# Two loads on two queues in place of one, for the last 15 full loads of a row-mean kernel

## The chip, the cores and the metric

The kernel runs on one core of one Trainium2 chip. The metric is the time of one execution on the device, in microseconds (us). Times named below are medians of several executions; a profile is one further execution, with its own time.

## The reference

```python
def setup_inputs():
    return {"x": np.random.randn(64, 256, 8192).astype(np.float32)}

def reference(x):
    return np.mean(x, axis=2)
```

There are 64 x 256 = 16,384 rows of 8,192 float32 (32 KB each), 536.87 MB in all, and one mean for each row comes out.

## The kernel before

**Rows and partitions.** Each of the 128 SBUF partitions owns 128 rows (`OWN`), in three zones of 95, 17 and 16 rows per partition. `rows_of(n, k)` is the slice of x with the own rows n to n+k-1 of every partition; in a zone these lie one behind the other in memory, so a slice of two rows is one run of 64 KB for each partition.

**Loads and buffers.** There are 63 full loads (`NB`), numbered g = 0 to 62. Each brings two rows per partition (128 x 64 KB, 8.39 MB) into one of three buffers, `bufs[g % 3]`, 64 KB per partition each. Load 0 comes in three pieces (lines 108 to 112), loads 1 and 2 at line 114, loads 3 to 47 in a loop of 15 rounds of three (line 121), and loads 48 to 62 one by one (line 127). All are issued by SyncE (SP) on its DMA queue. Before load g is issued, SP waits until the reduction of load g-3 has freed the buffer (`free_sems`).

**Reductions.** VectorE (DVE) waits for load g (`in_sems`), sums its two rows in one tensor_reduce of 128 x 16384 and frees the buffer. Loads 0 to 59 are reduced in a loop (line 168), loads 60 and 61 at line 178, and load 62 as two halves-sums (line 151, one for each row) that tell `owned_sem` when they are done.

**The tail.** The last two rows of each partition come in five chunks, which get smaller (line 133): 4,560, 2,240, 768, 368 and 256 KB. SP issues all five once load 60 has been reduced; the first four go into buffer 0, the last into `fin`. DVE sums the first chunk's full row and its own share of the next ones (line 151), ScalarE (ACT) sums its own share of the first four (line 207), and one last DVE sum over `fin` gives the last mean. GpSimd (POOL, line 97) scales all other sums once `owned_sem` has reached 4, that is after the two halves-sums of load 62, the reduction of load 61 and the sum of the first chunk's row. SP then issues the two stores of `scaled` (line 136), waits for the last DVE sum and issues the store of `ends` (line 140).

**Order.** Every engine runs its own list in the order written. ACT has nothing to do before the first chunk has landed; its list begins with the loading of its function table. The semaphores named are the only ties between engines.

## Time and profile before

| | |
|---|---|
| Median of 3 executions | 1243.22 us (1243.2 to 1243.32) |
| The profiled execution's own time | 1243.06 us |
| Its span, first to last instruction | 1241.7 us |
| Input read | 536.87 MB, 432 GB/s over the span |
| DVE busy | 1084.1 us (87%) |
| ACT busy | 5.2 us |
| POOL busy | 2.9 us |

What lies between the span and the execution's own time is 1.36 us. Engine names in the profile: DVE is VectorE, ACT is ScalarE, POOL is GpSimd, SPq is SyncE's list of DMA issues. "L168" is line 168 of the kernel. A row of the timeline gives start, duration, engine, line, operation, output<-input with partitions x elements, and in square brackets how long the engine had been idle and what ended that. The DMA share is the mean busy share of 16 DMA engines; a packet is one piece of a transfer that the profile records on one of them.

### The profile page before, as it was taken

What the parts mean: (1) busy time and instruction counts of PE and PEld (TensorE: products, weight loads), DVE (VectorE), ACT (ScalarE), POOL (GpSimd) and SP (SyncE); (2) the same over time, 40 slices, a digit from 0 to 9 for tenths busy, and PEclk for the clock granted to TensorE, in tenths of its full rate; (3) what the DMA queues carried; (4) which work ended last, traced back from release to release, by engine and by line L of the source; (5) the groups of instructions that cost most, each with busy time, mean ns of one, the idle gap of its engine ahead of it and who ended that gap; (6) DMA issues with size and microseconds to landing.
All of it is one profiled execution on the core that took longest, in us unless ns stands there. A gap on an engine that the chain in (4) does not pass through costs nothing. (4 is left out here: it accounts for less than half of the span.)

```text
span 1241.7 us, 549 instructions
## 1 busy us (share of the span) xinstructions
DVE 1084.1 (87%) x76; ACT 5.2 (0%) x9; POOL 2.9 (0%) x9
## 2 busy tenths in 40 slices
DVE  2898988989889898898898988989889898898987
ACT  0000000000000000000000000000000000000001
POOL 0000000000000000000000000000000000000000
DMA  9999999999999999999999999999999999999998
GB/s 405 439 439 439 439 435 410 439 439 439 439 439 433 412 439 439 439 439 439 426 418 439 439 439 439 439 422 422 439 439 439 439 439 422 422 439 439 439 439 374
DMA packets 10512, 536.94 MB, mean 432 GB/s; under 512 B 1552, under 2 KB 1552, under 8 KB 1936
## 3 DMA queue, kind: packets, MB, share of 16 engines
q1 hardware_dynamic: 10512, 536.94, 99.9%
HBM read 536.87 MB, written 0.07 MB: 432 GB/s over the span
## 5 line engine op out<-in xcount | busy, mean ns | idle before, releaser
L168 DVE TENSOR_REDUCE res<-buf 128x16384 f32 x60 | 1033.2, 17220 | 146.5 <-DVEq L167 146.5
L178 DVE TENSOR_REDUCE res<-buf 128x2 f32<-128x16384 f32 x2 | 34.4, 17220 | 4.0 <-DMA buf<-in_x_dram 4.0
L151 DVE CUSTOM_DVE_ANT_0 buf<-buf 128x4096 f32<-128x4096 f32 (+3 forms) x6 | 16.0, 2672 | 5.4 <-DMA buf<-in_x_dram 5.4
L207 ACT ACTIVATE buf<-buf 128x928 f32<-128x928 f32 (+3 forms) x4 | 3.6, 897 | 1233.7 <-DMA buf<-in_x_dram 1233.7
L97 POOL TENSOR_SCALAR scaled<-res 128x94 f32<-128x94 f32 (+2 forms) x3 | 2.4, 784 | 1235.0 <-DVE res L151 1234.8
L207 ACT ACT_TABLE_LOAD x1 | 1.3, 1283 | 0.7 <-PEq L221 0.7
L207 ACT ACTIVATION_READ_ACCUMULATOR buf<-buf 128x1 f32 x4 | 0.7, 187 | 0.0
L151 DVE CUSTOM_DVE_ANT_0 fin<-fin 128x260 f32<-128x260 f32 x1 | 0.4, 429 | 0.3 <-DMA fin<-in_x_dram 0.3
L97 POOL TENSOR_SCALAR ends<-res 128x15 f32<-128x15 f32 x1 | 0.3, 264 | 0.1
L151 DVE DVE_READ_ACCUMULATOR2_ANT res<- 128x1 f32 x3 | 0.3, 84 | 0.0
L151 DVE DVE_READ_ACCUMULATOR2_ANT fin<- 128x1 f32 x3 | 0.2, 81 | 0.0
L221 POOL MEMSET const-bfloat16-1.0<- 128x1 bf16 x1 | 0.1, 102 | 0.0
L221 POOL MEMSET const-uint8-127<- 128x1 uint8 x1 | 0.1, 102 | 0.0
L88 POOL MEMSET fin<- 128x1 f32 x1 | 0.1, 99 | 0.3 <-POOLq L221 0.3
L221 POOL MEMSET const-float32-0.0<- 128x1 f32 x1 | 0.1, 99 | 0.2 <-issue 0.2
L221 POOL MEMSET const-float32-1.0<- 128x1 f32 x1 | 0.1, 99 | 0.0
L151 DVE DVE_READ_ACCUMULATOR2_ANT ends<- 128x1 f32 x1 | 0.1, 82 | 0.0
## 6 DMA issues: line engine op xcount, KB each, us to landing
buf<-in_x_dram SPq DMA_DIRECT2D x1, 4560.0 KB, 32.2
buf<-in_x_dram SPq DMA_DIRECT2D x1, 4096.0 KB, 20.6
buf<-in_x_dram SPq DMA_DIRECT2D x1, 3072.0 KB, 11.4
buf<-in_x_dram SPq DMA_DIRECT2D x1, 2240.0 KB, 37.1
buf<-in_x_dram SPq DMA_DIRECT2D x1, 1024.0 KB, 4.6
buf<-in_x_dram SPq DMA_DIRECT2D x62, 40.3
buf<-in_x_dram SPq DMA_DIRECT2D x1, 768.0 KB, 38.5
buf<-in_x_dram SPq DMA_DIRECT2D x1, 368.0 KB, 39.0
```

Of the source, the lines that this page charges most:

```text
L88: eng.memset(part(NPART - 1), 0.0).then_inc(part_d, 1)
L97: eng.tensor_scalar(dst, src, inv, None, op0=mybir.AluOpType.mult).then_inc(pool_sem, 1)
L151: eng.tensor_tensor_reduce(ap[:, 0:n], ap[:, 0:n], ap[:, n : 2 * n], scale=scale, scalar=0.0, op0=ADD, op1=ADD, accum_out=to,).then_inc(do ...
L168: eng.tensor_reduce(sums[:, bass.ds(i, 1), b, :], bufs[b][:].rearrange("p (j l) -> p j l", j=2), X, ADD,).then_inc(free_sems[b], 1)
L178: eng.tensor_reduce(res[:, 2 * g : 2 * g + 2], bufs[b][:].rearrange("p (j l) -> p j l", j=2), X, ADD,).then_inc(free_sems[0] if b == 0 els ...
L207: eng.activation(ap, ap, COPY, accum_out=part(c)).then_inc(part_a, 1)
L221: nc = _bacc.Bacc("TRN2", target_bir_lowering=False, num_devices=1)
```

## The change

The loads 48 to 62 come as two loads of one row each. SP issues the one for the pair's first row, into the first half of the buffer, and ACT the one for the second row, into the second half. Both wait for the same event as before (the reduction of load g-3), by new semaphores `late_free_sems`, and both count up one new semaphore for the buffer, `late_in_sems`, for which DVE waits in steps of 32. The 15 issues of ACT stand ahead of all its other work. DVE's loop runs 15 rounds (loads 0 to 44) and not 20; the reductions of loads 45 to 61 are written out one by one. The chunks, the sums and the stores are as before, with their waits on the new semaphores.

```diff
+        late_in_sems = [sem(f"late_in_sem{i}") for i in range(NBUF)]
+        late_free_sems = [sem(f"late_free_sem{i}") for i in range(NBUF)]
...
-        eng.wait_ge(free_sems[0], LOADS0 + 1)
+        eng.wait_ge(late_free_sems[0], LOADS0 + 1)
         eng.wait_ge(owned_sem, 4)
...
         for g in range(PAIRS0 + 1, NB):
             b = g % NBUF
-            eng.wait_ge(free_sems[b], (g - PAIRS0 - 1) // NBUF + 1)
-            eng.dma_start(bufs[b][:], rows_of(first_row(g), 2)).then_inc(in_sems[b], 16)
-        eng.wait_ge(free_sems[0], LOADS0 + 1)
+            eng.wait_ge(late_free_sems[b], (g - PAIRS0 - 1) // NBUF + 1)
+            eng.dma_start(bufs[b][:, 0:L], rows_of(first_row(g), 1)).then_inc(
+                late_in_sems[b], 16
+            )
+        eng.wait_ge(late_free_sems[0], LOADS0 + 1)
...
-        with eng.Fori(0, NB // NBUF - 1) as i:
+        with eng.Fori(0, ROUNDS) as i:
...
-        for b in range(NBUF):
-            g = NB - NBUF + b
-            eng.wait_ge(in_sems[b], 16)
-            if b < 2:
+        for g in range(ROUNDS * NBUF, NB):
+            b = g % NBUF
+            if g <= PAIRS0:
+                eng.wait_ge(in_sems[b], 16)
+            else:
+                eng.wait_ge(late_in_sems[b], 32 * ((g - PAIRS0 - 1) // NBUF + 1))
+            if g < NB - 1:
                 eng.tensor_reduce(
...
-                ).then_inc(free_sems[0] if b == 0 else owned_sem, 1)
+                ).then_inc(late_free_sems[b] if g < NB - 2 else owned_sem, 1)
...
         eng = nc.scalar
+        for g in range(PAIRS0 + 1, NB):
+            b = g % NBUF
+            eng.wait_ge(late_free_sems[b], (g - PAIRS0 - 1) // NBUF + 1)
+            eng.dma_start(bufs[b][:, L : 2 * L], rows_of(first_row(g) + 1, 1)).then_inc(
+                late_in_sems[b], 16
+            )
         for c in range(4):
             eng.wait_ge(chunk_sems[c], 16)
```

More of the change, by code (lines that the diff above doesn't have):

```diff
@@ L83, in bass_global_avg_pool_1d_kernel, with rows_of @@
         part = lambda n: fin[:, LAST + n : LAST + n + 1]
+        def rows_of(n, k):
+            z = 2 if n >= FROM[2] else 1 if n >= FROM[1] else 0
+            return zone[z][:, (n - FROM[z]) * L : (n - FROM[z] + k) * L]
         eng = nc.gpsimd
         eng.memset(part(NPART - 1), 0.0).then_inc(part_d, 1)
-        eng.wait_ge(free_sems[0], LOADS0 + 1)
+        eng.wait_ge(late_free_sems[0], LOADS0 + 1)
         eng.wait_ge(owned_sem, 4)
@@ L102, in bass_global_avg_pool_1d_kernel @@
         eng = nc.sync
-        def rows_of(n, k):
-            z = 2 if n >= FROM[2] else 1 if n >= FROM[1] else 0
-            return zone[z][:, (n - FROM[z]) * L : (n - FROM[z] + k) * L]
         a, z = rows_of(ZONE[0] - 1, 1), rows_of(ZONE[0], 1)
```

## The prediction

> **What bounds the kernel now.** I read the page first: shares, DMA queue, groups.

> ```profile
> span 1241.7 us, 549 instructions
> DVE 1084.1 (87%) x76; ACT 5.2 (0%) x9; POOL 2.9 (0%) x9
> DMA packets 10512, 536.94 MB, mean 432 GB/s; under 512 B 1552, under 2 KB 1552, under 8 KB 1936
> q1 hardware_dynamic: 10512, 536.94, 99.9%
> L168 DVE TENSOR_REDUCE res<-buf 128x16384 f32 x60 | 1033.2, 17220 | 146.5 <-DVEq L167 146.5
> ```

> The DMA engines are busy 99.9% of the span, on the one queue that there is; DVE needs 17.22 us for a load and waits before each. The timeline around the first changed load, and its issues, show the rhythm.

> ```profile
> 909.31 38.92 SPq L127 DMA_DIRECT2D buf<-in_x_dram  x3
> 911.37 17.22 DVE L168 TENSOR_REDUCE res<-buf 128x16384 f32 x1 [2.09 <-DVEq L167]
> 930.65 17.22 DVE L168 TENSOR_REDUCE res<-buf 128x16384 f32 x1 [2.06 <-DVEq L167]
> 949.96 17.22 DVE L168 TENSOR_REDUCE res<-buf 128x16384 f32 x1 [2.09 <-DVEq L167]
> ...
> 1162.48 17.22 DVE L168 TENSOR_REDUCE res<-buf 128x16384 f32 x1 [2.07 <-DVEq L167]
> ```

> The last row is load 59, DVE's first three are loads 46, 47 and 48. From 47 to 59 it is 231.83 us for 12 loads, so 19.32 us each, or 434.2 GB/s. Load 48 is issued at 909.31 (load 45 is done) and load 46 lands at 911.37, so 2.06 us of load 46 and the whole of load 47 (19.32 us) are still ahead of it on the queue: the queue always holds over 21 us of work. So neither the issue nor DVE sets the pace, the stream of bytes does.

> The end decides, as the timeline of the last 60 us shows.

> ```profile
> 1181.58 17.22 DVE L178 TENSOR_REDUCE res<-buf 128x2 f32<-128x16384 f32 x1 [1.89 <-DMA buf<-in_x_dram]
> 1198.83 1.75 SPq L133 DMA_DIRECT2D buf<-in_x_dram  x4
> 1200.62 0.43 SPq L133 DMA_DIRECT2D fin<-in_x_dram  x1
> 1200.96 17.22 DVE L178 TENSOR_REDUCE res<-buf 128x2 f32<-128x16384 f32 x1 [2.16 <-DMA buf<-in_x_dram]
> 1220.27 4.42 DVE L151 CUSTOM_DVE_ANT_0 buf<-buf 128x4096 f32<-128x4096 f32 x1 [2.09 <-DMA buf<-in_x_dram]
> ...
> 1224.62 4.42 DVE L151 CUSTOM_DVE_ANT_0 buf<-buf 128x4096 f32<-128x4096 f32 x1
> 1228.96 0.08 DVE L151 DVE_READ_ACCUMULATOR2_ANT res<- 128x1 f32 x1
> 1231.01 4.43 DVE L151 CUSTOM_DVE_ANT_0 buf<-buf 128x4096 f32<-128x4096 f32 x1 [1.97 <-DMA buf<-in_x_dram]
> ...
> 1235.62 2.51 POOL L97 TENSOR_SCALAR scaled<-res 128x94 f32<-128x94 f32 x3 [1234.80 <-DVE res L151]
> 1236.35 1.66 DVE L151 CUSTOM_DVE_ANT_0 buf<-buf 128x1440 f32<-128x1440 f32 x1 [0.91 <-DMA buf<-in_x_dram]
> ...
> 1238.24 0.69 DVE L151 CUSTOM_DVE_ANT_0 buf<-buf 128x496 f32<-128x496 f32 x1 [0.22 <-DMA buf<-in_x_dram]
> 1238.50 0.82 SPq L136 DMA_DIRECT2D out_dram<-scaled  x2
> ...
> 1239.14 0.41 DVE L151 CUSTOM_DVE_ANT_0 buf<-buf 128x240 f32<-128x240 f32 x1 [0.20 <-DMA buf<-in_x_dram]
> ...
> 1239.83 0.43 DVE L151 CUSTOM_DVE_ANT_0 fin<-fin 128x260 f32<-128x260 f32 x1 [0.26 <-DMA fin<-in_x_dram]
> ...
> 1240.29 0.33 SPq L140 DMA_DIRECT2D out_dram<-ends  x1
> ```

> After load 62 (landed at 1220.27) DVE is only just ahead of the chunks: it ends load 62 at 1229.0 and the first chunk lands at 1231.01. Loads 61 and 62 have 2.09 us to spare against the stream and the chunk 1.97. So DVE work that slips by more than about 4.1 us before the chunks sets the end in place of the stream.

> **The change part by part.** *Bytes and packets.* The bytes stay. The page's packets are one per partition and transfer: 62 loads of 128 x 64 KB, the smaller ones, and 16 completions for each of the 73 transfers (73 x 144 = 10,512). Thirty transfers in place of 15 add 15 x 144, so 12,672. Does a 32 KB packet go slower than one of 64 KB? The chunks' sizes:

> ```profile
> buf<-in_x_dram SPq DMA_DIRECT2D x1, 4560.0 KB, 32.2
> ...
> buf<-in_x_dram SPq DMA_DIRECT2D x1, 2240.0 KB, 37.1
> ```

> The nearest row is the first chunk, 36,480 B to a partition: 4.67 MB between 1220.27 and 1231.01, or 434.8 GB/s. The next one (17,920 B) takes 1231.01 to 1236.35 for 2.29 MB, 429.6 GB/s, 1.1% less. I take 0 by the nearer row; the far bound is 1.1% of the some 299 us from 911 to 1210, +3.3 us. The lower bound is 0, as the engines are already busy 99.9%.

> *Issues.* ACT's 15 issues are new. SP's cost 0.33 to 0.43 us each; ACT has nothing else before 1231.01, and issues the last one when load 59 is reduced, before 1200. Its function table load moves behind that,

> ```profile
> 0.72 1.28 ACT L207 ACT_TABLE_LOAD   x1 [0.72 <-PEq L221]
> ```

> and is still some 30 us ahead of the first chunk: 0 on the path. Were that cover gone, it would cost 1.3 us. SP's own issues are as many as before, and queued behind each of its waits there is only the next load. DVE's shorter loop: its gaps are waits for data, 2.06 to 2.16 us each, so 0.

> *The order of the bytes: the term that costs.* Each DMA engine now has two queues to draw from. At 909.31, load 48b (the second row, on ACT's queue) is issued with that queue empty, while 48a stands behind load 47 on SP's queue. Here the trace doesn't show how an engine shares itself between queues, only what it handles at a time:

> ```profile
> 950.00:960.00 10.00, 10.00 (x1) 0.00 (x0) 0.00 (x0) 1.00 0.97 419
> 960.00:970.00 10.00, 7.84 (x2) 0.00 (x0) 0.00 (x0) 1.00 0.97 419
> ```

> In 10 us, 419 GB/s is 4.19 MB, or 16 engines x 4 packets of 64 KB: the engines go in step, and a 64 KB packet (2.41 us, an eighth of 19.32) is recorded one after another, with a share not over one. I therefore take turns by packet: one of 47 (2.41 us), one of 48b (1.21 us), eight times. Both are done 28.98 us after 46, so 47 lands 9.66 us late, at 940.3, and DVE idles 11.7 us where it idled 2.06. In the time 49b has joined ACT's queue (issued at 928.6). From 940.3, 48a and 49b share, each half, and 48 lands 19.32 us later, 9.66 us late like 47. So ACT's queue stays one row ahead: each load g is complete only when b of load g+1 is in as well. No byte is lost, since SP's queue is never empty, but every load from 47 to 61 is complete 9.66 us late.

> [...] No trace here has two queues.

> *The end.* Load 61 lands at 1200.96 + 9.66 = 1210.62, and its reduction ends at 1227.86. 62a follows alone and lands at 1220.3 as before, since all bytes of 61 and 62 are in by then; the chunks land as before. DVE does 62's rows from 1227.86 (two times 4.35 us, the spacing of 1220.27 and 1224.62) to 1236.56. The first chunk's sum starts there and not at 1231.01: 5.55 us late. POOL, SP's two stores and what is behind them move with it: 1238.50 + 5.55 = 1244.05, two issues to 1244.87, and `ends` goes out then, not at 1240.29: +4.6 us. DVE's own chain (4.35 + 1.67 + 0.7 + 0.4 + 0.43 us from 1236.56) ends at 1244.1 and is no longer. In general, load 61 late by x costs x - 5.1: 4.1 us at DVE and 1.0 between the stores and the last issue, 0 below that.

> *How much of the lead holds.* ACT's next row is issued 2.06 us before the load in progress is complete, and an issue needs about as long to bring bytes:

> ```profile
> 0.73 0.39 SPq L108 DMA_DIRECT2D buf<-in_x_dram  x1
> ...
> buf<-in_x_dram SPq DMA_DIRECT2D x1, 1024.0 KB, 4.6
> ```

> 1.05 MB take 2.41 us of these 4.6, so 2.2 us are start and completion, against 2.06. ACT's queue can run empty for an instant, and SP then gets one more 32 KB packet in: the lead would be 8.45 us, and the price +3.4. It can't shrink by the same again, since a shorter lead gives DVE's release more time. I take the middle, +4.0: the profiled execution 1243.06 + 4.0 = 1247.1, and from the median of the runs, 0.16 us above it, 1247.2 us.

> **The rivals.**

> *Equal shares by bytes, the lead lost (no change).* If engines switch within a packet, 47 gets half the rate for as long as ACT has rows: 48b, then 49b (issued at 928.6, before 48b is through). 47 then lands at 911.4 + 38.6 = 950, 19.3 us late, and 50b can't be issued before 47 is reduced at 967.2. SP's 48a and 49a have the engines alone until 969.3; after that 50a and 50b start level. DVE runs without a wait and regains 2.1 us a load, over some ten loads, so at 61 x is near 0. The point from which it decides: whether 49b comes to bear before 47 is done. [...] Against it: the step of whole packets above. Time 1243.2; at worst 1.5 us of idle engines at 969. Chance 0.16.

> *Turns of a whole transfer, and a missed turn (no change).* ACT's next row comes 2.2 - 2.06 us too late for its turn; SP then sends a whole row alone and the lead of 9.66 us is gone in one step: 1243.2. [...] Against it: the page counts every piece of a transfer as a packet. Chance 0.08.

> *One queue after all.* If both issuers feed one ring in order of issue (the page has only q1, with one issuer), a and b follow each other and all is as before: 1243.2. Chance 0.05.

> *SP's queue first.* If an engine serves ACT's queue only when SP's is empty, 62b comes after the chunks, at 1239.8. The first chunk's sum then starts at 1239.8 + 8.7 = 1248.5, 17.5 us late, +16.5: 1259.7. Nothing in the profile speaks for it. Chance 0.04.

> *Two streams go slower.* Taking turns costs up to the 3.3 us above besides the lead: 1250.5. Chance 0.05.

> *Two queues go faster.* DVE would allow 10% (17.24 against 19.32). 1% over 299 us is 3 us: 1240.2. The 99.9% speak against it. Chance 0.03.

> **How the numbers follow.** The forecast has 0.59; its own range is 1246.3 to 1248. No change in three ways has 0.29, 0.05 is slower by rate, 0.04 by SP first, 0.03 faster. Below 0.2% (2.5 us) no measurement here can tell a change from none. So slower 0.68, same 0.29, faster 0.03. The range takes in no change and the slower rate up to 1250: 1242.9 to 1250, and leaves out some 0.1.

> **What would show it.** Packets 12,672 on two queues. DVE's wait before load 47 is 11.7 us (21 by equal shares, 2.1 by one queue), and later waits near 2.1; with equal shares there would be none for some ten loads. ACT's issues land sooner after issue than SP's of the same load, by up to 20 us. Load 61 starts near 1210, the first chunk's sum near 1236 without a wait for data, and the `ends` store goes out behind POOL's scaling. The forecast is wrong if load 61 starts before 1206, or if loads come other than 19.3 us apart.

## The result, and the profile after

The changed kernel takes 1247.83 us (median of 6, 1247.55 to 1248.07), the kernel before, on the same chip, 1243.22 us (6 runs, 1243.17 to 1243.32). The ratio is 1.0037, with a 95% interval of 1.0027 to 1.0048: 4.6 us slower. The profiled execution took 1248.01 us.

The page of the changed kernel, its span, packets and queues:

```profile
span 1246.7 us, 519 instructions
...
DMA packets 12672, 536.94 MB, mean 431 GB/s; under 512 B 1792, under 2 KB 1792, under 8 KB 2176
...
q1 hardware_dynamic: 10512, 474.03, 87.9%
q10 hardware_dynamic: 2160, 62.92, 11.7%
```

ACT has a queue of its own, q10, with 15 transfers of 144 packets and 62.92 MB. The packets are the 12,672 forecast. The timeline where the change begins, rows as before (start, duration, engine and line, in brackets the idle time before it):

```profile
909.30 86.14 SPq L129 DMA_DIRECT2D buf<-in_x_dram  x5
909.31 86.17 ACTq L213 DMA_DIRECT2D buf<-in_x_dram  x5
911.36 17.22 DVE L185 TENSOR_REDUCE res<-buf 128x2 f32<-128x16384 f32 x1 [2.08 <-DMA buf<-in_x_dram]
940.32 17.22 DVE L185 TENSOR_REDUCE res<-buf 128x2 f32<-128x16384 f32 x1 [11.74 <-DMA buf<-in_x_dram]
959.74 17.22 DVE L185 TENSOR_REDUCE res<-buf 128x2 f32<-128x16384 f32 x1 [2.20 <-DMA buf<-in_x_dram]
977.87 17.22 DVE L185 TENSOR_REDUCE res<-buf 128x2 f32<-128x16384 f32 x1 [0.91 <-DMA buf<-in_x_dram]
997.19 17.22 DVE L185 TENSOR_REDUCE res<-buf 128x2 f32<-128x16384 f32 x1 [2.10 <-DMA buf<-in_x_dram]
```

The DVE rows are loads 46 to 50. Load 47 is complete at 940.32 and not at 930.65: 9.67 us late, by the wait of 11.74. The wait of 0.91 before load 49 is short by 1.2 us: there ACT's lead shrinks by one packet of 32 KB (1.21 us), once.

How the 16 engines share themselves between the two queues can be read from the DMA view of short windows (packets, MB, share of the engines): first 913 to 916.6 us, while load 47 is still on its way, then 943 to 945.5.

```profile
q1 hardware_dynamic: 16, 1.05, 67.2%
q10 hardware_dynamic: 16, 0.52, 33.7%
...
q1 hardware_dynamic: 16, 0.52, 48.5%
q10 hardware_dynamic: 16, 0.52, 48.5%
```

After load 49 the rhythm is even again, and the lateness stays to the end, as the timeline of the last 60 us shows:

```profile
1190.82 17.22 DVE L185 TENSOR_REDUCE res<-buf 128x2 f32<-128x16384 f32 x1 [2.11 <-DMA buf<-in_x_dram]
...
1210.21 17.22 DVE L185 TENSOR_REDUCE res<-buf 128x2 f32<-128x16384 f32 x1 [2.17 <-DMA buf<-in_x_dram]
...
1227.35 4.42 DVE L155 CUSTOM_DVE_ANT_0 buf<-buf 128x4096 f32<-128x4096 f32 x1
...
1231.89 0.98 ACT L220 ACTIVATE buf<-buf 128x928 f32<-128x928 f32 x1 [41.48 <-DMA buf<-in_x_dram]
...
1236.04 4.42 DVE L155 CUSTOM_DVE_ANT_0 buf<-buf 128x4096 f32<-128x4096 f32 x1
...
1243.21 0.54 POOL L103 TENSOR_SCALAR ends<-res 128x15 f32<-128x15 f32 x1
...
1243.78 0.82 SPq L140 DMA_DIRECT2D out_dram<-scaled  x2
1244.64 0.43 SPq L144 DMA_DIRECT2D out_dram<-ends  x1
```

Load 61 starts at 1210.21 (before: 1200.96). The sums of load 62 and of the first chunk have no bracket: DVE went from one to the next without a wait. ACT's share of the first chunk starts at 1231.89, when the chunk lands, so the stream is only 0.9 us later there than before (1231.01); DVE takes the chunk up at 1236.04, 4.15 us after it has landed. POOL and SP come behind DVE, and the store of `ends` goes out at 1244.64 and not at 1240.29. The chain that ended last has changed over with it: a DMA landing before (`fin`), POOL's scaling now.

```profile
DMA buf<-in_x_dram 20%; DVE res L185 8%; DVE buf L155 1%; POOL scaled L103 0%; POOL ends L103 0%; SPq L123 0%; DVE res L155 0%; POOLq L96 0%
```

### The profile page after: what moved, and what is told of

Same layout as the page of the kernel before. It is cut to its first block, busy times and chain, and to the rows that moved or that the text cites. A ratio compares the mean times of both kernels' runs of the same rounds, so it can differ in the third digit from the quotient of the medians.

```text
span 1246.7 us, 519 instructions
## 1 busy us (share of the span) xinstructions
DVE 1083.7 (87%) x76; ACT 5.2 (0%) x9; POOL 3.2 (0%) x9
## 2 busy tenths in 40 slices
DMA packets 12672, 536.94 MB, mean 431 GB/s; under 512 B 1792, under 2 KB 1792, under 8 KB 2176
## 3 DMA queue, kind: packets, MB, share of 16 engines
q1 hardware_dynamic: 10512, 474.03, 87.9%
q10 hardware_dynamic: 2160, 62.92, 11.7%
## 5 line engine op out<-in xcount | busy, mean ns | idle before, releaser
L172 DVE TENSOR_REDUCE res<-buf 128x16384 f32 x45 | 774.9, 17220 | 115.2 <-DVEq L171 115.2
L185 DVE TENSOR_REDUCE res<-buf 128x2 f32<-128x16384 f32 x17 | 292.7, 17220 | 44.6 <-DMA buf<-in_x_dram 44.6
L103 POOL TENSOR_SCALAR scaled<-res 128x94 f32<-128x94 f32 (+2 forms) x3 | 2.3, 778 | 1240.0 <-DVE res L155 1239.8
## 6 DMA issues: line engine op xcount, KB each, us to landing
buf<-in_x_dram SPq DMA_DIRECT2D x16, 4096.0 KB, 23.9
buf<-in_x_dram ACTq DMA_DIRECT2D x15, 4096.0 KB, 40.8
buf<-in_x_dram SPq DMA_DIRECT2D x1, 4560.0 KB, 23.8
buf<-in_x_dram SPq DMA_DIRECT2D x1, 2240.0 KB, 28.7
buf<-in_x_dram SPq DMA_DIRECT2D x1, 1024.0 KB, 4.5
```

The source lines that it names most:

```text
L103: eng.tensor_scalar(dst, src, inv, None, op0=mybir.AluOpType.mult).then_inc(pool_sem, 1)
L172: eng.tensor_reduce(sums[:, bass.ds(i, 1), b, :], bufs[b][:].rearrange("p (j l) -> p j l", j=2), X, ADD,).then_inc(free_sems[b], 1)
L185: eng.tensor_reduce(res[:, 2 * g : 2 * g + 2], bufs[b][:].rearrange("p (j l) -> p j l", j=2), X, ADD,).then_inc(late_free_sems[b] if g < N ...
```

## The experiments

The theory: an engine takes turns by packet between its two queues, so ACT's row of the next load passes the load in progress, each load from 47 on is complete some 9 us late, and only the end pays, because DVE then has too little time before the chunks. The first four runs change one side of that each; the others put the split on a single load.

**Both rows on SP's queue.**

```diff
             eng.dma_start(bufs[b][:, 0:L], rows_of(first_row(g), 1)).then_inc(
                 late_in_sems[b], 16
             )
+            eng.dma_start(bufs[b][:, L : 2 * L], rows_of(first_row(g) + 1, 1)).then_inc(
+                late_in_sems[b], 16
+            )
...
         eng = nc.scalar
-        for g in range(PAIRS0 + 1, NB):
...
```

> Both rows of loads 48 to 62 are issued by SP, one behind the other; ACT issues nothing. Theory (ACT's queue runs one row ahead, so that load 61 is late by 9.3 us at the end): with one queue there is no lead; DVE waits 2.1 us before load 47, load 61 starts at 1201 to 1201.8, and the time is 1243.2 to 1244.0 us. The upper end if the slower rhythm of the changed kernel (19.36 us a load against 19.32) comes from the 15 more transfers, the lower if it comes from the second queue. Rival A (the smaller packets or the 15 more transfers cost it): 1247 to 1248 us, as in the changed kernel.

Measured: 1243.8 us, ratio 1.0005 (0.9995 to 1.0015). The timeline's loads 47, 48, 60 and 61:

```profile
930.68 17.22 DVE L188 TENSOR_REDUCE res<-buf 128x2 f32<-128x16384 f32 x1 [2.07 <-DMA buf<-in_x_dram]
950.08 17.22 DVE L188 TENSOR_REDUCE res<-buf 128x2 f32<-128x16384 f32 x1 [2.18 <-DMA buf<-in_x_dram]
...
1182.43 17.22 DVE L188 TENSOR_REDUCE res<-buf 128x2 f32<-128x16384 f32 x1 [2.18 <-DMA buf<-in_x_dram]
1201.76 17.22 DVE L188 TENSOR_REDUCE res<-buf 128x2 f32<-128x16384 f32 x1 [2.10 <-DMA buf<-in_x_dram]
```

No stall before load 47, and rival A falls: the pieces alone don't bring the 4.6 us. From 48 to 60 it is 232.35 us for 12 loads, 19.363 us each; the changed kernel has 232.34 us from load 49 to 61, the same, and the kernel before had 19.319. So a load in two transfers, with packets of half the size, costs 0.044 us more, on one queue as on two. The packet records of the two traces (the kernel before and this run) divide that: on an engine, packets of 64 KB start 2.4141 us apart and packets of 32 KB 1.2094 us, so 16 small ones take 0.038 us longer than 8 large ones, and the step at the end of a transfer is 0.006 us longer than the others. Most of it lies with the smaller packets, then, and little with the additional transfer. Load 61 is 0.80 us later here (1201.76 against 1200.96), but 0.24 us of that is there already at load 42 (834.33 against 834.09), before the first changed load; the other 0.56 us is 13 loads at 0.044. In the whole time that is about the 0.6 us seen (1243.8 against 1243.17 for the kernel before on the same chip), which the interval of the ratio can't tell from nothing.

**ACT's first row held back by one load.**

```diff
         eng = nc.scalar
         for g in range(PAIRS0 + 1, NB):
             b = g % NBUF
+            if g == PAIRS0 + 1:
+                eng.wait_ge(late_free_sems[1], 1)
```

> As the changed kernel, but ACT holds its first row (48b) back until load 46 has been reduced, 19.3 us later; all 30 loads stay on two queues. Theory: when 48b is issued, load 47 has only some 2 us left, so the queues start level and stay so; DVE's wait before load 47 is 3.3 us or less, load 61 starts at 1201 to 1203, and the time is 1243.2 to 1244.2 us. Rival B (each load on two queues costs some 0.3 us, in issue, landing or rate, 15 times): 1247 to 1248 us.

Measured: 1243.87 us, ratio 1.0006 (0.9997 to 1.0016). All 30 half loads are still on two queues, and of the loss about as much is left as on one queue (0.7 us against 0.6), so rival B falls. The wait before 47 is 2.06 us as in the kernel before. The queues didn't start quite level: load 48 waits 4.38 us, and load 61 starts at 1203.99, a microsecond past what was expected. Now SP's queue is ahead, by two packets of 1.21 us: from 929.9 to 932.35 us the DMA view has 1.05 MB on q1 and nothing on q10. Each load is then complete when ACT's row is, some 2.3 us late. That much fits in the slack before the chunks: the first chunk's sum starts at 1232.28.

**Load 47 in 32 KB packets as well.** SP's loop runs one round less, and its last three loads are written out:

```diff
...
+        for g in range(ROUNDS * NBUF, PAIRS0 + 1):
+            b = g % NBUF
+            eng.wait_ge(free_sems[b], 1).then_inc(free_sems[b], -1)
+            if g < PAIRS0:
...
+            else:
+                for j in range(2):
+                    eng.dma_start(
+                        bufs[b][:, j * L : (j + 1) * L], rows_of(first_row(g) + j, 1)
+                    ).then_inc(in_sems[b], 16)
...
-                eng.wait_ge(in_sems[b], 16)
+                eng.wait_ge(in_sems[b], 16 if g < PAIRS0 else 32)
```

> As the changed kernel, but load 47 comes in packets of 32 KB too (its two rows as two loads on SP's queue). Theory (turns by packet): 47 now gets half the engines and not two thirds. 48b takes turns with 47's first row and 49b, issued at 928.6, with its second, so load 47 lands 19.3 us late: DVE idles 21 us before it (11.7 in the changed kernel). ACT's queue then stands empty until 47 is reduced, the lead is gone, DVE runs with no wait for some ten loads, and the time is 1243.2 to 1244.5 us: the larger stall gives the better end. Rival C (turns by bytes or by time, whatever the packet): nothing changes, a wait of 11.7 us and 1247 to 1248 us. Rival D (an early stall is lost time): about 1257 us.

Measured: 1244.01 us, ratio 1.0006 (0.9997 to 1.0016). The timeline from load 46 on:

```profile
911.31 17.22 DVE L197 TENSOR_REDUCE res<-buf 128x2 f32<-128x16384 f32 x1 [2.09 <-DMA buf<-in_x_dram]
948.78 137.10 DVE L197 TENSOR_REDUCE res<-buf 128x2 f32<-128x16384 f32 x8 [20.25 <-DMA buf<-in_x_dram]
1086.54 17.22 DVE L197 TENSOR_REDUCE res<-buf 128x2 f32<-128x16384 f32 x1 [0.66 <-DMA buf<-in_x_dram]
```

Only load 47 has changed, into two transfers with packets of half the size, and it now lands 18.1 us late (948.78 against 930.65), one packet of 1.2 us short of two rows. So the turns were counted in packets here, not in bytes (18.1 us late with 32 KB packets in load 47, 9.67 with 64 KB); rival C falls. By turns of a whole transfer, 47 would have come 9.66 us late, or 19.3 if 49b had caught its turn, and not 18.1; the windows above, with one packet from each queue in turn, put those out too. The row "x8" is eight reductions on end, loads 47 to 54: DVE works off the stall, ACT's queue has lost its lead for lack of free buffers, and load 61 starts at 1202.76. The largest stall of all these runs, the wait for the very first load aside, costs nothing that the time can show; rival D falls.

**ACT sums the second row of load 62.**

```diff
-                for j in range(2):
+                for j in range(1):
                     halves(
...
         eng = nc.scalar
...
+        eng.wait_ge(late_in_sems[2], 32 * LOADS0)
+        ap = bufs[2][:, L : 2 * L]
+        eng.activation(
+            ap, ap, COPY, accum_out=res[:, 2 * NB - 1 : 2 * NB]
+        ).then_inc(owned_sem, 1)
```

> As the changed kernel, but ACT sums the second row of load 62 (8192 elements, some 8 us by its 1.54 us for 1600) after both rows have landed at 1221, and DVE only the first: 4.35 us less on DVE at the end. Theory (DVE's work before the chunks slips past them): load 47 and 61 are as late as in the changed kernel, 61 at 1210.2, but DVE starts the first chunk's sum at 1231.9, when it lands, and the time is 1243.6 to 1244.4 us. Rival E (the stream itself ends later by 4 us): 1247 to 1248 us.

Measured: 1243.79 us, ratio 1.0005 (0.9995 to 1.0015). The timeline at load 61, and what follows:

```profile
1210.08 17.22 DVE L185 TENSOR_REDUCE res<-buf 128x2 f32<-128x16384 f32 x1 [2.18 <-DMA buf<-in_x_dram]
1220.99 7.03 ACT L218 ACTIVATE buf<-buf 128x8192 f32<-128x8192 f32 x1 [30.70 <-DMA buf<-in_x_dram]
1227.22 4.42 DVE L155 CUSTOM_DVE_ANT_0 buf<-buf 128x4096 f32<-128x4096 f32 x1
1231.76 0.98 ACT L225 ACTIVATE buf<-buf 128x928 f32<-128x928 f32 x1 [3.64 <-DMA buf<-in_x_dram]
1231.76 4.42 DVE L155 CUSTOM_DVE_ANT_0 buf<-buf 128x4096 f32<-128x4096 f32 x1
```

Load 61 is as late as in the changed kernel (1210.08), and yet the time is that of the run on one queue (1243.8): with 4.35 us of work taken off DVE it meets the first chunk as it lands, at 1231.76. So 4.0 of the 4.6 us were DVE's lateness at the chunks; the 0.6 us that stay are as many as on one queue.

**The split on one load alone.** SP issues whole loads but for one; ACT issues the second row of that one.

```diff
-            eng.dma_start(bufs[b][:, 0:L], rows_of(first_row(g), 1)).then_inc(
-                late_in_sems[b], 16
+            k = 1 if g == NB - 1 else 2
+            eng.dma_start(bufs[b][:, 0 : k * L], rows_of(first_row(g), k)).then_inc(
+                late_in_sems[b], 16 if k == 1 else 32
             )
...
-        for g in range(PAIRS0 + 1, NB):
+        for g in [NB - 1]:
```

This is load 62; in the other three, `NB - 1` is `NB - 2`, `NB - 3` and `PAIRS0 + 1`.

> Only load 62 comes on two queues; loads 48 to 61 are whole loads on SP's queue, as before the change. Theory: 62b is issued when load 59 is reduced (1179.7) and takes turns with the packets of load 61, so 61 lands 9.66 us late, near 1210.6, and the time is 1247.3 to 1248.0 us: one split load costs as much as 15. Rival B (each split load costs 0.3 us): 1243.2 to 1243.6 us.

> Only load 61 comes on two queues. Theory: 61b takes turns with the packets of load 60, so 60 lands 9.66 us late, near 1191.3; 61 is complete on time and DVE regains 2.1 us at 61 and 2.1 us at 62 against the stream. DVE starts the first chunk's sum at 1234.4, 3.4 us late, and the time is 1245.4 to 1246.1 us, between the 1248.26 of the split of load 62 alone and the 1243.31 of load 48 alone. Rival F (the price hangs on load 62 being in two parts, not on when DVE is through): 1243.2 us.

> Only load 60 comes on two queues. Theory: 59 lands 9.66 us late, near 1172.2, DVE regains 2.1 us at each of 60, 61 and 62, starts the first chunk's sum some 1.5 us late, and the time is 1243.6 to 1244.2 us. Rival F: 1243.2 us.

> Only load 48 comes on two queues; loads 49 to 62 are whole loads on SP's queue. Theory: load 47 is 9.66 us late (DVE idles 11.7 us before it), but 48 needs only its first row then and lands on time, DVE catches up, and the time is 1243.0 to 1243.5 us: a lead that isn't there at the end costs nothing. Rival D (DVE's stall of 10 us is lost): 1252 us; rival B: 1243.5 us, which this run can't tell from the theory.

| load that is split | time, us | ratio (95%) | first chunk's sum starts |
|---|---|---|---|
| 62 | 1248.26 | 1.0042 (1.0027 to 1.0056) | 1236.59 |
| 61 | 1245.97 | 1.0022 (1.0012 to 1.0032) | 1234.31 |
| 60 | 1243.85 | 1.0006 (0.9996 to 1.0016) | 1232.01 |
| 48 | 1243.31 | 1.0001 (0.9992 to 1.0011) | 1231.26 |

The timelines, one fence for each kernel from load 62 to load 48, with the late load and the first chunk's sum:

```profile
1210.76 17.22 DVE L186 TENSOR_REDUCE res<-buf 128x2 f32<-128x16384 f32 x1 [11.83 <-DMA buf<-in_x_dram]
...
1236.59 4.42 DVE L156 CUSTOM_DVE_ANT_0 buf<-buf 128x4096 f32<-128x4096 f32 x1
```

```profile
1191.37 34.35 DVE L186 TENSOR_REDUCE res<-buf 128x2 f32<-128x16384 f32 x2 [11.76 <-DMA buf<-in_x_dram]
...
1234.31 4.42 DVE L156 CUSTOM_DVE_ANT_0 buf<-buf 128x4096 f32<-128x4096 f32 x1
```

```profile
1171.94 51.47 DVE L186 TENSOR_REDUCE res<-buf 128x2 f32<-128x16384 f32 x3 [11.76 <-DMA buf<-in_x_dram]
...
1232.01 4.42 DVE L156 CUSTOM_DVE_ANT_0 buf<-buf 128x4096 f32<-128x4096 f32 x1
```

```profile
940.33 85.72 DVE L186 TENSOR_REDUCE res<-buf 128x2 f32<-128x16384 f32 x5 [11.73 <-DMA buf<-in_x_dram]
...
1231.26 4.42 DVE L156 CUSTOM_DVE_ANT_0 buf<-buf 128x4096 f32<-128x4096 f32 x1 [2.00 <-DMA buf<-in_x_dram]
```

Each time the load ahead of the split one is late, with the same wait of 11.7 to 11.8 us. Then DVE runs on end, "x2", "x3", "x5", and each load that follows gives 2.1 to 2.3 us back: the chunk's sum starts at 1236.59, 1234.31, 1232.01. One split of load 62 costs as much as 15 splits and a little more, and one of load 48 nothing that can be measured, so rival B falls once more, and rival F with the split of load 61. The split of load 62 came 0.26 us above what was expected, and 0.4 us above the changed kernel: its load 61 is 0.55 us later (1210.76 against 1210.21). A single split has no later turn to miss, so it keeps the packet that the changed kernel loses at load 49, and it has the slower rhythm of the smaller packets for one load only; whether these two make up the 0.55 us was not tested.

No run beats the kernel before, and none showed a way to: where DVE kept up, the stream of bytes set the end, as before (the one queue's share is 99.9% in the kernel before and in the run on one queue).

## Why the prediction was right

*What bounds the kernel.* Right. The stream sets the pace, and the only slack that counts is DVE's before the chunks. The run with ACT's sum moves that slack alone and gets all but 0.6 us of the loss back.

*Turns by packet, the lead.* Right, and to the tenth: load 47 at 940.3 forecast, 940.32 measured, a wait of 11.7 forecast, 11.74 measured. That landing alone would fit longer turns too. That the unit is the packet was an inference; the short windows above (16 packets from each queue, one for each engine) and the run with 32 KB packets in load 47 (18.1 us late) showed it: a turn was one piece of 32 KB or 64 KB.

*How much of the lead holds.* Of the two ends the lower came out: one packet was lost, at load 49, and none after. Load 61 was 9.25 us late, of which 0.80 is what the run on one queue has too; 8.45 us are the lead, as worked out for that end.

*Bytes and packets, at 0.* A term of the sum that was mis-sized. The nearest row, a chunk with packets of 36 KB, gave 0; measured were 0.044 us a load, 0.038 of them for the smaller packets, and some 0.56 us by load 61. The far bound of 3.3 us held.

*The end.* The form x - 5.1 gives 9.25 - 5.1 = 4.15 us; the store of `ends` went out 4.35 us later. POOL's last scaling took 0.54 us where it took 0.26, which is about the rest. The span grew by 5.0 us, 0.65 more than that, behind the last issue: the store landed in 2.0 us and not 1.4. That store now follows 0.86 us behind the two others and not 1.8; whether this is why was not tested. So +4.0 was forecast, and +4.6 came in the medians and +4.95 in the profiled executions. That it is this near is in part luck. The lead brought 3.4 us and not 4.0; against that stand 0.8 us by which load 61 is late on one queue too, 0.2 us of POOL and 0.65 us behind the last issue, none of which was in the sum.

*The issues.* Right at 0. ACT's last issue is at 1188.7, its table load follows at 1189.13, 42 us ahead of the first chunk.

*Which row lands first.* The prediction looked for ACT's rows to land sooner after their issue than SP's, by up to 20 us. The profile's page says the reverse in its issue lines (a median of 40.8 us for ACT's loads, 23.9 for SP's), but both rows of a load count up one semaphore, so these lines may not tell them apart. The packet records agree with the forecast: the completions of 48b go out at 939.8 us and those of 48a, issued at the same time, at 959.1.

*The rivals.* Equal shares by bytes and one queue are excluded by load 47's landing in the two runs, whole transfers by the short windows; SP first too, for by it load 47 would have landed on time. Slower or faster streams: the rhythm on two queues is that on one, to 0.001 us.

## What to carry to other kernels

Here a transfer issued on an empty second queue didn't wait for what was issued earlier on the first: it took every other turn at once and made the older transfer 9.67 us late, though the first chunk landed only 0.9 us later. So when loads are spread over two queues, ask what each new transfer passes, and whether the consumer of what it passes has slack left; start the queues level, or nearly so, as the run with ACT held back did (0.7 us lost there, 4.6 in the changed kernel). The size of the packets set each queue's share (67.2% for 64 KB against 33.7% for 32 KB), but no run here used it to keep the older transfer on time. A stall of the consumer in the middle of a stream (11.73 us before load 47, with load 48 alone split) cost nothing that could be measured here, because the stream ran on, the consumer was faster (17.22 us a load against 19.32) and enough loads were left to regain it, at 2.1 to 2.3 us a load; the same stall before load 61 (11.83 us) cost 5.1 us, and the slack at the end took up the rest.

## What was not expected of the hardware

A load in two transfers of 32 KB packets took 0.044 us longer than one in 64 KB packets, on one queue as on two (19.363 us against 19.319): 0.038 us for the packets, 0.006 for the additional transfer. A transfer's completion took its turn too: the last data packet of load 47 on q1 ended at 938.8 us at the latest in the changed kernel, its completions went out at 939.8, after one more packet of q10, and the load landed at 940.32. ACT's sum with accumulation over 128 x 8192 took 7.03 us, where 1.54 us for 1600 elements gave 7.9. POOL's 128 x 15 scaling took 0.26 us in the kernel before, where it starts 0.03 us ahead of a DVE sum (1238.21 against 1238.24), and 0.54 in the changed one. In three runs where it started while a DVE sum ran, it ended about 0.2 us after DVE went on from that sum to the read of its accumulator: at 1243.75 against 1243.56 in the changed kernel, at 1239.89 against 1239.69 in the run with ACT held back, at 1239.70 against 1239.50 in the split of load 60. No run tested why.
